# Zero blocks written by GpSimd instead of turned by TensorE, and five small re-orderings, in a one-core macaron block with stick-breaking attention

## The chip, the cores and the metric

The kernel runs on one core of a Trainium2 chip. Its time is the device time of one launch in microseconds (us), the median of several runs. Five engines work side by side, each through its own queue in order: PE (TensorE, matmuls and transposes), DVE (VectorE), ACT (ScalarE), POOL (GpSimd) and SP (SyncE, which issues the DMAs). Semaphores link them. "L1098" is line 1098 of the kernel before.

## The reference

One macaron block on x of 1024 rows by 1024 columns, all in float32: a gated FFN, stick-breaking attention with 16 heads of width 64, a second gated FFN.

```python
x = x + 0.5 * swiglu(rms_norm(x, n1), wi1, wo1)
x = x + stick_breaking_attention(rms_norm(x, mix_norm), w_qkv, q_gain, k_gain, w_o)
x = x + 0.5 * swiglu(rms_norm(x, n2), wi2, wo2)

# in the attention, for each head, t = row, s = column, s < t:
z = einsum("qd,kd->qk", rms_norm(q), rms_norm(k)) / sqrt(64)
# A[t,s] = sigmoid(z[t,s]) * prod over s<j<t of (1 - sigmoid(z[t,j]))
o = A @ v
```

## The kernel before

**Precision.** A float32 product is made of three matmuls: each operand is split into a high part (ACT copies it with rounding, L196) and a low part (DVE or POOL subtracts, L197), and high by high, low by high and high by low are added up in one bank of the accumulator (L308, L309, L310). For the weights w of the attention and for q and k a form with two matmuls is used (`th` and `tl`, `kh_s` and `kl_s`).

**Stages.** FFN 1 takes the first 620 us, a transition the next 140, the attention with the output projection behind it the time from about 700 to 1330, FFN 2 the rest.

**Attention.** The 16 heads run as 8 pairs (p = 0 to 7), some 63.5 us each. A pair has four units: `a` (head 1, rows 512 to 1023), `b` (head 0, rows 0 to 511), `c` (head 1, rows 0 to 511) and, already for the pair after it, `d` (head 0, rows 512 to 1023). Heads, rows and columns are stored mirrored, so that the product over j is a prefix scan. A unit does this:

- `scores` (L1058 to L1073): for each block `tb` of 128 rows, two matmuls make the scores in a bank `bz` (512 columns, or 512, 384, 256, 128 for the short blocks beside the diagonal). ACT takes two sigmoids of them, beta into `w` and 1 - beta back into the bank. A DVE scan (L1066) makes the running product, with `first` (zeros with a diagonal of ones) as the lower bound. POOL multiplies beta by it (L1073, the weights `w`), after a memset of the first column (L1071).
- `values`: for each group of 128-column blocks `sb`, `turn` transposes 128x128 pieces of `w` through the identity into a bank `bt` (L1098), and `split` makes `th` (ACT) and `tl` (DVE). `apply` multiplies them by v (L1116) into a bank `bo`. The last group of a unit holds two `sb`: one with two pieces, one with a single piece. The single piece is widened to two by a transpose of zeros from `first[:, P:2P]`, so that the matmul of `apply` has 256 columns for either. `th` and `tl` have two buffers each, so a group's tiles come free when the group two before it has been applied.

Between these stand the *fills*: 24 steps of the next pair's q, k, v projection (`qkv`, banks `bq`, L308 to L310), three matmuls of 384 columns for each of four 128-row slices of the contraction. When a projection tile is complete, ACT takes its squares and copies (L980, L981, L984), DVE reduces (L986), and after each four tiles `rsqrt` runs as one ACT instruction (`rs_a`, L207) and ten small DVE instructions (L208 to L212), followed by `r` (L992) and `f` (L1003). From `r` POOL scales k (L996, L999). `f` is the scale of the sigmoids. `prep_q` and `prep_k` then turn q or k (L1016) and multiply by the gains: ACT makes `q_s` or the high part `kh_s` (L1020), DVE the rest (`q_s` again, or `kl_s`, L1021).

**Order.** Every step goes into a list `plan` with a number for its place, and the list is sorted by that number. A unit's length is in `PARTS` (10, 14, 21, 16), and `put("c", 17.5, f)` means 17.5 after the start of `c`. `spread` sets steps at equal distances. Where an instruction of a queue stands follows from this list, except that `following(mark)` issues an instruction behind a named other one. The output weights (`out_weights`, tiles `raw`, 128x1024) are loaded during pair 6; the first two are copied on ACT at one place, near the end of unit `d` and the start of `a`. For the first pair no earlier unit exists, so its fills, `steps[12:]`, are spread over the numbers -30 to -11.

Of the kernel before, what the change touches and what calls it, by code (L numbers as in the profile page):

```python
# [9 lines left out]
F32 = mybir.dt.float32  # L10
F32R = mybir.dt.float32r
I32 = mybir.dt.int32
AF = mybir.ActivationFunctionType
# [100 lines left out]
def macaron_kernel(ctx, tc, x, g1, w1_in, w1_out, gm, w_qkv, gq, gk, w_o, g2, w2_in, w2_out, out):  # L114
# [801 lines left out]
    with ExitStack() as stack:  # L916
# [39 lines left out]
        def qkv(p, state):  # L956


            def start(half):
                if half:  # L960
                    state["v"] = pl[f"vst{p % 2}"].tile([P, NT, 4, DH], F32R, name="vst", bufs=1)
                state["qk", half] = pl[f"qk{half}"].tile([P, 4, 6, DH], F32, name=f"qk{half}", bufs=1)
                state["ssq"] = pl["sq"].tile([P, 4, 4], F32, name="ssq", bufs=1)

            def step(half, i, ks):
                if i == 0 and ks.start == 0:
                    start(half)
                if ks.start == 0:
                    state["ps"] = bank("bq")
                room, ps = state["ps"][:, 3 * P :], state["ps"][:, : 3 * P]  # L970
                wh, wl = state["wq"]
                t = rows(half * 4 + i)
                mm3(ps, [((xh[:, k, t], xl[:, k, t]), (wh[k], wl[k])) for k in ks], ks.start == 0, ks.stop == KD)
                if ks.stop == KD:
                    finish(half, i, ps, room)

            def finish(half, i, ps, room):
                qk, ssq, vst = state["qk", half], state["ssq"], state["v"]
                sq = pl["sq"].tile([P, 4, DH], F32, name="sq")
                act.activation(sq.rearrange("p a b -> p (a b)"), ps[:, : 2 * P], AF.Square)  # L980
                act.activation(qk[:, i, 0:4].rearrange("p a b -> p (a b)"), ps[:, : 2 * P], AF.Copy)  # L981
                pv = ps[:, 2 * P :].rearrange("p (a b) -> p a b", b=DH)
                vh = vst[:, half * 4 + i, 0:4:3, :]
                state["evacuated"] = act.activation(vh, pv, AF.Copy).ins  # L984
                dve.tensor_tensor(vst[:, half * 4 + i, 1:3, :], pv, vh.bitcast(F32), op=ALU.subtract)
                dve.tensor_reduce(out=ssq[:, i, :], in_=sq, axis=AX.X, op=ALU.add)  # L986
                if i < 3:
                    return
                y = rsqrt(pl["sq"], ssq.rearrange("p a b -> p (a b)"), 1.0 / DH, room[:, :16])
                y = y.rearrange("p (a b) -> p a b", b=4)  # L990
                r = state["r"] = pl["sq"].tile([P, 4, 4], F32, name="r", bufs=1)
                dve.tensor_scalar(r[:, :, 0:2], y[:, :, 2:4], 1.0, None, op0=ALU.mult)  # L992

                rk = r[:, :, 0:1].unsqueeze(3).to_broadcast([P, 4, 2, DH])
                kv = qk[:, :, 2:3, :].to_broadcast([P, 4, 2, DH])
                pool_e.tensor_tensor(qk[:, :, 4:6, :], kv, rk, op=ALU.mult)  # L996
                for to in (2, 3):
                    rk = r[:, :, 1:2].to_broadcast([P, 4, DH])
                    pool_e.tensor_tensor(qk[:, :, to, :], qk[:, :, 3, :], rk, op=ALU.mult)  # L999

                f = state["f", half] = pl["sq"].tile([P, 2, 4, 2], F32, name=f"f{half}")
                for n, c in enumerate((0.125, -0.125)):
                    dve.tensor_scalar(f[:, n], y[:, :, 0:2], c, None, op0=ALU.mult)  # L1003

            return [
                partial(step, half, i, ks)
                for half in (1, 0)
                for i in range(4)
                for ks in (range(0, 3), range(3, 6), range(6, KD))
            ]  # L1010
# [27 lines left out]
        def scores(state, hd, half):  # L1038

            w = state["w", hd, half] = {}  # L1040

            def step(tb, kb):
                L = T - tb * P
                if kb == half:
                    t = pl["w"].tile([P, T - tb % 4 * P], F32, name=f"w{hd}{tb % 4}", bufs=1)

                    om = t[:, L : 2 * L] if half else pl["om"].tile([P, T], F32, name="om")
                    state["om"], w[tb] = om, t[:, :L]
                om, wt = state["om"], w[tb]
                q = state["q", hd, half][:, (tb % 4) * P : (tb % 4 + 1) * P]  # L1050
                s0 = max(tb * P, kb * NHALF)
                n = (kb + 1) * NHALF - s0
                c0 = s0 - tb * P
                off = P if n == P else 0
                z = bank("bz")
                keys = slice(s0 - off - kb * NHALF, NHALF)
                for i in range(2):
                    pe.matmul(z[:, : off + n], q, state["k", hd, kb][i][:, keys], start=i == 0, stop=i == 1)  # L1058

                z = z[:, off : off + n]  # L1060
                for to, sign in ((wt[:, c0 : c0 + n], 0), (z, 1)):
                    marks["scored"] = act.activation(  # L1062
                        to, z, AF.Sigmoid, scale=state["f", half][:, sign, tb % 4, hd : hd + 1]
                    ).ins
                least = first[:, P : P + 1].to_broadcast([P, n]) if c0 else first[:, :n]
                dve.tensor_tensor_scan(  # L1066
                    om[:, c0 : c0 + n], z, least, initial=om[:, c0 - 1 : c0] if c0 else 0.0,
                    op0=ALU.mult, op1=ALU.max,
                )
                if c0 == 0:  # L1070
                    pool_e.memset(wt[:, 0:1], 0.0)  # L1071
                c1 = max(c0, 1)
                marks["weighed"] = pool_e.tensor_tensor(  # L1073
                    wt[:, c1 : c0 + n], wt[:, c1 : c0 + n], om[:, c1 - 1 : c0 + n - 1], op=ALU.mult
                ).ins

            return [partial(step, tb, kb) for tb in range(half * 4, half * 4 + 4) for kb in range(half, 2)]

        def values(state, p, hd, half):
# [8 lines left out]
            def turn(sbs):  # L1088
                w = state["w", hd, half]
                tp = bank("bt")  # L1090
                n, now_at = 0, tc.cur_priority
                for sb in sbs:
                    for i in range(max(blocks(sb), 2)):
                        c = (sb - tb0 - i) * P

                        src = w[tb0 + i][:, c : c + P] if i < blocks(sb) else first[:, P : 2 * P]
                        tc.cur_priority = now_at
                        pe.transpose(tp[:, n : n + P], src, ident)  # L1098
                        n += P
                th, tl = now[sbs] = [pl["th"].tile([P, NHALF], F32R, name=n) for n in ("th", "tl")]  # L1100
                split(tp[:, :n], th[:, :n], tl[:, :n])

            def apply(sbs):
# [76 lines left out]
        first = pl["first"].tile([P, NHALF], F32, name="first", bufs=1)  # L1180
        pool_e.memset(first, 0.0)
        dve.tensor_copy(first[:, :P], ident)
        spread(steps[12:], -30.0, -11.0)
        for p in range(-1, NP):
            this = states[p] if p >= 0 else None
            nxt = states[p + 1] if p < NP - 1 else None
# [19 lines left out]
            if nxt is not None:  # L1206
                if p >= 0:
                    fills = qkv(p + 1, nxt)
                    for part, span in PARTS.items():
                        for i in range(FILLS[part]):  # L1210
                            t = (span - (3.0 if part == "d" else 0.0)) * (i + 0.5) / FILLS[part]
                            put(part, t - 0.1 if (part, i) == ("a", FILLS["a"] - 1) else t, fills.pop(0))
                put("c", 15.0, partial(prep_q, nxt, 1))
                put("c", 17.5 if p >= 0 else 20.0, partial(prep_k, nxt, 0, 1))
                put("d", 8.0, partial(prep_k, nxt, 1, 1))
            if this is not None:
                put("a", 5.0, partial(prep_q, this, 0))
# [10 lines left out]
            if p == NP - 2:  # L1228

                def note(i, f):  # L1230
                    pool_e.tensor_tensor(seen[:, i : i + 1], f(), f(), op=ALU.mult)

                put("c", 14.0, partial(note, 0, lambda s=nxt: s["qk", 1][:, 0, 4, 0:1]))
                put("d", 1.0, partial(note, 1, lambda s=nxt: s["k", 0, 1][1][:, 0:1].bitcast(F32)))
                put("c", 10.0, partial(load_o, 1))
                put("d", 15.5, lambda: spots.append(tc.cur_priority))
            if p == NP - 1:
                put("a", 2.5, partial(load_o, 0))
                for at, _, _ in SHARES:
                    put(*at, lambda: spots.append(tc.cur_priority))  # L1240
# [10 lines left out]
    with pools(*PROJECTION) as pl:  # L1251
# [3 lines left out]
        def out_weights(c, k, rooms):  # L1255
# [9 lines left out]
                there = seen[:, k // 2 : k // 2 + 1] if k < 4 else wo[-1][1][:, 0:1].bitcast(F32)  # L1265
                pool_e.tensor_tensor((l_ if k < 4 else h_)[:, 0:1], there, there, op=ALU.mult)
            if c is HALVES[0]:
                split(raw, h_, l_, lane(f"wo{k // 2}"))
            else:
                with following(marks["scored"] if k < 4 else None):  # L1270
                    act.activation(h_, raw, AF.Copy)
# [113 lines left out]
```

## Time and profile before

| | us |
|---|---|
| median of 3 runs | 1916.08 (1914.53 to 1917.19) |
| profiled execution, its own time | 1914.4 |
| its span | 1912.5 |
| PE busy | 1897.4 (99%) |
| DVE, POOL, ACT busy | 1237.0, 1127.8, 979.9 |

The span runs from the first to the last instruction. The 1.9 us between span and time of the profiled execution lie around it. The granted clock was 1.0. In views of single instructions a row gives start, duration, engine, line and operation, output <- inputs, and in brackets how long the engine sat idle and who ended it. Matmuls are pipelined, so a row's duration overlaps the next one; what an instruction takes from PE is the step from its start to the next start.

### The profile page before, as it was taken

How to read it: one execution, taken by the hardware profiler on the slowest of the kernel's cores; microseconds unless marked ns; L12 is line 12 of the kernel's file. 1: busy time of each engine (PE TensorE's matmuls, PEld its weight loads, DVE VectorE, ACT ScalarE, POOL GpSimd, SP SyncE). 2: the span in 40 equal slices, each digit the busy share in tenths (PEclk: the TensorE clock that was granted, in tenths of full speed). 3: DMA queues.
4: the chain of work that ended last, by engine and by line, in shares of the span. 5: the costliest groups of instructions: out<-in, count | busy, mean ns of one | idle time of the engine just before them, and what ended most of it. 6: DMA issues, size and time to landing. Idle time of an engine off the chain costs nothing.

```text
span 1912.5 us, 26698 instructions
## 1 busy us (share of the span) xinstructions
PE 1897.4 (99%) x9362; PEld 1624.8 (85%) x9362; DVE 1237.0 (65%) x1713; ACT 979.9 (51%) x1794; POOL 1127.8 (59%) x999
## 2 busy tenths in 40 slices
PE   9999999999999999999999999999999999999999
PEld 8878888888888899999999897788888888888887
DVE  6856445535775758888888777568456445548645
ACT  7433433334335458878888876344433443434332
POOL 6766666656556746656665564215666666654554
PEclk9999999999999999999999999999999999999999
DMA  6233323338897411011111152612333323369983
GB/s 204 89 115 111 105 87 117 105 115 278 307 354 259 138 34 45 32 47 45 45 37 42 50 170 74 225 50 74 103 110 116 105 83 117 110 229 342 331 268 138
DMA packets 168982, 258.65 MB, mean 135 GB/s; under 512 B 11664, under 2 KB 82320, under 8 KB 168848
## 3 DMA queue, kind: packets, MB, share of 16 engines
q1 hardware_dynamic: 168704, 256.95, 39.3%
q8 instruction: 73, 1.20, 0.3%
q14 instruction: 61, 0.50, 0.1%
q10 hardware_dynamic: 144, 0.00, 0.0%
HBM read 197.14 MB, written 59.77 MB: 134 GB/s over the span
## 4 chain that ended last, share of the span: by engine, by line
PE 86%; DVE 8%; ACT 3%; issue 1%; POOL 1%; DMA 0%; SPq 0%; DVEq 0%; ACTq 0%; POOLq 0%
PE ka L308 6%; PE ka L309 6%; PE ka L310 6%; PE bq L308 4%; PE bq L309 4%; PE bq L310 4%; PE kc L308 4%; PE kc L309 4%; PE kc L310 4%; PE ma L310 4%; PE ma L309 4%; PE ma L308 4%; PE kb L308 4%; PE kb L309 4%; PE kb L310 4%; PE mb L310 3%
## 5 line engine op out<-in xcount | busy, mean ns | idle before, releaser
L197 POOL TENSOR_TENSOR rp<-raw,rp 128x1024 fp32r<-128x1024 f32 x84 | 213.7, 2551 | 168.0 <-ACT rp L196 157.0
L197 POOL TENSOR_TENSOR u<-sf,u 128x512 fp32r<-128x512 f32 x160 | 227.6, 1425 | 136.2 <-ACT u L196 136.2
L197 POOL TENSOR_TENSOR u<-raw,u 128x512 fp32r<-128x512 f32 x128 | 187.5, 1467 | 152.5 <-ACT u L196 151.7
L196 ACT ACTIVATE u<-sf 128x512 fp32r<-128x512 f32 x160 | 100.8, 630 | 204.7 <-PE kb L309 87.1
L1073 POOL TENSOR_TENSOR w<-w,om 128x512 f32<-128x512 f32 (+4 forms) x128 | 140.9, 1104 | 107.6 <-DVE om L1066 94.0
L446 DVE TENSOR_TENSOR h<-h 128x512 f32<-128x512 f32 x110 | 135.4, 1234 | 85.8 <-POOL h L554 85.1
L308 PE MATMUL bq<-wqh,xh 128*128 128x384 f32 x512 | 174.4, 341 | 0.4
L196 ACT ACTIVATE rp<-rh 128x1024 fp32r<-128x1024 f32 (+1 forms) x78 | 76.4, 983 | 189.9 <-issue 60.2
L309 PE MATMUL bq<-wql,xh 128*128 128x384 f32 x512 | 172.2, 336 | 0.0
L310 PE MATMUL bq<-wqh,xl 128*128 128x384 f32 x512 | 172.1, 336 | 0.0
L576 DVE TENSOR_TENSOR raw<-raw 128x1024 f32<-128x1024 f32 (+1 forms) x60 | 95.0, 1585 | 105.4 <-DMA raw<-w_out 91.7
L196 ACT ACTIVATE u<-raw 128x512 fp32r<-128x512 f32 x128 | 80.2, 630 | 149.8 <-PE ka L309 100.8
L308 PE MATMUL ka<-xh,u 128*128 128x512 f32 x352 | 137.2, 390 | 1.9 <-ACT s L499 1.9
L308 PE MATMUL ma<-rp 128*128 128x512 f32 x352 | 137.0, 389 | 0.0
L310 PE MATMUL ka<-xh,u 128*128 128x512 f32 x352 | 137.0, 389 | 0.0
L310 PE MATMUL ma<-rp 128*128 128x512 f32 x352 | 136.9, 389 | 0.0
L309 PE MATMUL ka<-xl,u 128*128 128x512 f32 x352 | 136.9, 389 | 0.0
L309 PE MATMUL ma<-rp 128*128 128x512 f32 x352 | 136.9, 389 | 0.0
L554 POOL TENSOR_TENSOR h<-h,g 128x512 f32<-128x512 f32 x80 | 113.0, 1412 | 35.1 <-DVE h L503 33.3
L1062 ACT ACTIVATE w<-bz,f 128x512 f32<-128x512 f32 (+1 forms) x192 | 113.1, 589 | 34.5 <-PE bz L1058 33.4
L475 DVE TENSOR_TENSOR sf<-raw 128x512 f32<-128x512 f32 x80 | 80.3, 1003 | 77.9 <-POOL u L197 77.9
L197 DVE TENSOR_TENSOR rp<-rh,rp 128x1024 fp32r<-128x1024 f32 (+1 forms) x70 | 109.7, 1585 | 21.9 <-ACT rp L196 19.6
(309 smaller groups left out, 5465.8 us busy)
## 6 DMA issues: line engine op xcount, KB each, us to landing
raw<-w_out SPq DMA_DIRECT2D x120, 512.0 KB, 5.7
raw<-w_in SPq DMA_DIRECT2D x86, 512.0 KB, 3.6
k<-h SPq DMA_DIRECT2D x154, 256.0 KB, 2.1
rh<-k SPq DMA_DIRECT2D x64, 512.0 KB, 6.2
raw_qkv<-w_qkv SPq DMA_DIRECT2D x64, 192.0 KB, 2.9
x_keep<-x SPq DMA_DIRECT2D x32, 256.0 KB, 3.4
x<-x_keep SPq DMA_DIRECT2D x32, 256.0 KB, 5.6
raw<-w_out SPq DMA_DIRECT2D x24, 256.0 KB, 4.6
```

Of the source, the lines that this page charges most:

```text
L196: first = act.activation(hi, raw, AF.Copy).ins
L197: return first, (engine or dve).tensor_tensor(lo, raw, hi.bitcast(F32), op=ALU.subtract).ins
L308: pe.matmul(dst, ah, bh, start=start and i == 0, stop=False, skip_group_check=onto)
L309: pe.matmul(dst, ah, bl, start=False, stop=False, skip_group_check=onto)
L310: pe.matmul(dst, al, bh, start=False, stop=stop and i == n - 1, skip_group_check=onto)
L446: dve.tensor_tensor(src, hb[of[0]], hb[of[1]], op=getattr(ALU, of[2]))
L475: dve.tensor_tensor(f[n], x, y, op=op)
L554: pool_e.tensor_tensor(h, h, gs[k], op=ALU.mult)
L576: dve.tensor_tensor(w[0], w[0], w[1], op=getattr(ALU, W_OF[m][2]))
L1062: marks["scored"] = act.activation(to, z, AF.Sigmoid, scale=state["f", half][:, sign, tb % 4, hd : hd + 1]).ins
L1073: marks["weighed"] = pool_e.tensor_tensor(wt[:, c1 : c0 + n], wt[:, c1 : c0 + n], om[:, c1 - 1 : c0 + n - 1], op=ALU.mult).ins
```

## The change

1. `turn` no longer transposes the zero block. Two POOL memsets write zeros into that block of `th` and `tl`, and `split` handles 384 columns instead of 512 in these groups (8 pairs by 4 units, so 32 groups).
2. `prep_k` of the next pair's (head 0, rows 512 to 1023) moves from 17.5 to 17.0 in `c`.
3. The fills of `d` are spread over 5.0 less than the unit's length instead of 3.0 less.
4. The first pair's fills are spread over -30 to -7.
5. The first two output-weight copies are issued behind a sigmoid at 3.0 and one at 9.0 in `b` of pair 6.
6. In the last pair, the scan of (head 1, `tb` 4), the first of `a`, is issued behind the instruction that makes `f`.

```diff
-                    dve.tensor_scalar(f[:, n], y[:, :, 0:2], c, None, op0=ALU.mult)
+                    state["rooted"] = dve.tensor_scalar(f[:, n], y[:, :, 0:2], c, None, op0=ALU.mult).ins
...
-                dve.tensor_tensor_scan(
+                with following(state["rooted"] if state is states[-1] and (hd, tb) == (1, 4) else None):
+                    dve.tensor_tensor_scan(
...
-                    for i in range(max(blocks(sb), 2)):
+                    for i in range(blocks(sb)):
...
-                        src = w[tb0 + i][:, c : c + P] if i < blocks(sb) else first[:, P : 2 * P]
-                        pe.transpose(tp[:, n : n + P], src, ident)
+                        pe.transpose(tp[:, n : n + P], w[tb0 + i][:, c : c + P], ident)
                         n += P
                 th, tl = now[sbs] = [pl["th"].tile([P, NHALF], F32R, name=n) for n in ("th", "tl")]
+                if blocks(sbs[-1]) == 1:
+                    for t in (th, tl):
+                        pool_e.memset(t[:, n : n + P].bitcast(F32), 0.0)
                 split(tp[:, :n], th[:, :n], tl[:, :n])
...
-        spread(steps[12:], -30.0, -11.0)
+        spread(steps[12:], -30.0, -7.0)
...
-                            t = (span - (3.0 if part == "d" else 0.0)) * (i + 0.5) / FILLS[part]
+                            t = (span - (5.0 if part == "d" else 0.0)) * (i + 0.5) / FILLS[part]
...
-                put("c", 17.5 if p >= 0 else 20.0, partial(prep_k, nxt, 0, 1))
+                put("c", 17.0 if p >= 0 else 20.0, partial(prep_k, nxt, 0, 1))
...
+                for k, at in ((0, ("b", 3.0)), (2, ("b", 9.0))):
+                    put(*at, lambda k=k: marks.update({f"wo{k}": marks["scored"]}))
...
-                split(raw, h_, l_, lane(f"wo{k // 2}"))
+                with following(marks.get(f"wo{k}")):
+                    act.activation(h_, raw, AF.Copy)
+                lane(f"wo{k // 2}").tensor_tensor(l_, raw, h_.bitcast(F32), op=ALU.subtract)
```

What this does to the queues is shown at three places. The first is POOL's queue near the end of a pair's `a`, where unit `a`'s last group is turned. `qk` is the projected q and k, `w_9938` (`w_9954` after the change) the weights of one row block. Before:

```order
435 L999 TENSOR_TENSOR qk_9417<-qk_9417,r 128x4x64
436 L1073 TENSOR_TENSOR w_9892<-w_9892 128x383
437 L999 TENSOR_TENSOR qk_9417<-qk_9417,r 128x4x64
438 L1071 MEMSET w_9938 128x1
439 L1073 TENSOR_TENSOR w_9938<-w_9938 128x255
440 L1071 MEMSET w_9993 128x1
```

After:

```order
469 L1074 TENSOR_TENSOR w_9908<-w_9908 128x383
470 L1072 MEMSET w_9954 128x1
471 L1103 MEMSET th 128x128
472 L1103 MEMSET tl 128x128
473 L1074 TENSOR_TENSOR w_9954<-w_9954 128x255
474 L1072 MEMSET w_10010 128x1
```

Two memsets of 128x128 now stand ahead of the 255-column weights. The second place is DVE's queue from the end of `c` to `d` and on to the next `a` of the same pair. `ssq` is the sum of squares, `kl_s` and `q_s` the finished k and q. Before, at the end of `c`, and then at the end of `d`:

```order
789 L1021 SCALAR_TENSOR_TENSOR q_s_9544<-bz,gq_sb,q_s_9544 64x512
790 L197 TENSOR_TENSOR tl<-bt,th 128x512
791 L197 TENSOR_TENSOR tl<-bt,th 128x384
792 L1021 SCALAR_TENSOR_TENSOR q_s_9547<-bz,gq_sb,q_s_9547 64x512
793 L1066 SCALAR_TENSOR_TENSOR om<-bz,first 128x128
794 L1021 SCALAR_TENSOR_TENSOR kl_s_9594<-bz,gk_sb,kh_s_9593 128x512
```

```order
807 L1066 SCALAR_TENSOR_TENSOR w_9767<-bz,first 128x256
808 L197 TENSOR_TENSOR tl<-bt,th 128x512
809 L197 TENSOR_TENSOR tl<-bt,th 128x384
810 L986 TENSOR_REDUCE ssq<-sq 128x4
811 L985 TENSOR_TENSOR vst<-bq,vst 128x128
812 L208 TENSOR_SCALAR bq<-rs_a 128x16
```

After, the same two places:

```order
789 L1021 SCALAR_TENSOR_TENSOR q_s_9558<-bz,gq_sb,q_s_9558 64x512
790 L197 TENSOR_TENSOR tl<-bt,th 128x512
791 L197 TENSOR_TENSOR tl<-bt,th 128x384
792 L1021 SCALAR_TENSOR_TENSOR kl_s_9589<-bz,gk_sb,kh_s_9588 128x512
793 L1021 SCALAR_TENSOR_TENSOR q_s_9561<-bz,gq_sb,q_s_9561 64x512
794 L1067 SCALAR_TENSOR_TENSOR om<-bz,first 128x128
```

```order
807 L1067 SCALAR_TENSOR_TENSOR w_9782<-bz,first 128x256
808 L986 TENSOR_REDUCE ssq<-sq 128x4
809 L985 TENSOR_TENSOR vst<-bq,vst 128x128
810 L208 TENSOR_SCALAR bq<-rs_a 128x16
811 L210 SCALAR_TENSOR_TENSOR rs_u<-bq,rs_a 128x16
812 L211 TENSOR_TENSOR rs_u<-rs_u,bq 128x16
813 L197 TENSOR_TENSOR tl<-bt,th 128x512
```

`kl_s` moved ahead of the second `q_s`, and the reduction with the start of `rsqrt` moved ahead of the two splits `tl`. The third place is ACT's queue at the start of pair 6's `a`. Before:

```order
1071 L196 ACTIVATE th<-bt 128x512
1072 L196 ACTIVATE raw<-raw 128x1024
1073 L1062 ACTIVATE w_11541<-bz,f_11086 128x512
1074 L1062 ACTIVATE bz<-bz,f_11086 128x512
1075 L196 ACTIVATE raw<-raw 128x1024
1076 L1121 ACTIVATE o_11145<-bo 64x512
```

After:

```order
1071 L196 ACTIVATE th<-bt 128x384
1072 L1062 ACTIVATE w_11565<-bz,f_11108 128x512
1073 L1062 ACTIVATE bz<-bz,f_11108 128x512
1074 L1124 ACTIVATE o_11167<-bo 64x512
1075 L1062 ACTIVATE w_11598<-bz,f_11108 128x384
1076 L1062 ACTIVATE bz<-bz,f_11108 128x384
```

The two copies `raw<-raw` are gone from this place; they stand in unit `b` of the pair now.

More of the change, by code (lines that the diff above doesn't have):

```diff
@@ L1065, in step @@
                 least = first[:, P : P + 1].to_broadcast([P, n]) if c0 else first[:, :n]
[L1066 to L1069, printed above, removed]
+                with following(state["rooted"] if state is states[-1] and (hd, tb) == (1, 4) else None):
+                    dve.tensor_tensor_scan(
+                        om[:, c0 : c0 + n], z, least, initial=om[:, c0 - 1 : c0] if c0 else 0.0,
+                        op0=ALU.mult, op1=ALU.max,
+                    )
                 if c0 == 0:
```

## The prediction

> **What bounds the kernel now.** I read the page's busy times first, then PE's waits by line and waited-for instruction, then the timeline at each place that the change touches.
>
> ```profile
> span 1912.5 us, 26698 instructions
> ## 1 busy us (share of the span) xinstructions
> PE 1897.4 (99%) x9362; PEld 1624.8 (85%) x9362; DVE 1237.0 (65%) x1713; ACT 979.9 (51%) x1794; POOL 1127.8 (59%) x999
> ```
>
> PE is idle for 15.1 us of the span, so time can leave in two ways only: PE issues less, or one of its few waits goes. Work taken off or put on the other engines counts only where PE waits for it. The waits (PE's line, what it waited for: total, times, longest):
>
> ```profile
> PE bz L1058 <- DVE kl_s L1021: 1.5, 7, 0.2
> PE mb L287 <- DVE x L622: 0.9, 2, 0.5
> PE bz L1016 <- POOL w L1071: 0.9, 1, 0.9
> PE bz L1058 <- DVE w L1066: 0.9, 3, 0.3
> PE bo L1116 <- DVE tl L197: 0.6, 1, 0.6
> PE bt L287 <- DVE xl L197: 0.5, 1, 0.5
> PE bo L1116 <- ACT th L196: 0.4, 1, 0.4
> ```
>
> Five of these seven rows lie in the attention, 4.3 us together. That is all that the moves can win, apart from restart losses that the idle column leaves out.
>
> **The zero turns.** 32 transposes leave PE. Their group, from the view by lines:
>
> ```profile
> L1098 PE MATMUL bt<-ident,first 128*128 128x128 f32 x32 | 8.7, 273 | 0.0
> ```
>
> 273 ns is the time through the array, and the next one starts long before. What one costs PE is the step between starts:
>
> ```profile
> 879.21 1.03 PE L1098 MATMUL bt<-ident,w 128*128 128x128 f32 x8
> ```
>
> Eight in 1.03 us, the last of them 0.27 long: (1.03 - 0.27) / 7 = 0.109 us a step. 32 x 0.109 = 3.5 us. It can be 8.7 at most, by the busy time, and 0 if PE waits right behind each of them. I take -3.5, since no idle time stands behind them in the group's row.
>
> The Trainium skill (TensorE: Matmul & The Clock Gate, Part 4: PE-mode transpose) gives a transpose about 275 ns in a kernel's context. The trace agrees with that as a duration, 273 ns. By the page alone the turns would be worth 32 x 0.275 = 8.8 us and the whole change 11.3 (an estimate), but the step measured here is 0.109.
>
> **The memsets.** 64 are added on POOL. The trace has one of that shape, and the place in a pair's `a` where two will stand:
>
> ```profile
> 0.73 0.20 POOL masks.py:197 MEMSET ident<- 128x128 f32 x1 [0.29 <-POOLq L1375]
> ```
>
> ```profile
> 900.50 0.74 POOL L1073 TENSOR_TENSOR w<-w 128x255 f32<-128x255 f32 x1 [0.57 <-DVE w L1066]
> ```
>
> 64 x 0.20 = 12.8 us of POOL, which is idle 41% of the span. At the shown place POOL idles 0.57 us for a scan, and two memsets take 0.40 of that. Behind them in POOL's queue stand the next weights, and PE's later turns wait for those. The memsets also wait themselves, for the apply two groups earlier to free `th` and `tl`. At this place that apply is the following row; it ends at 899.01, about 0.9 us before POOL would come to them, right ahead of its idle time.
>
> ```profile
> 898.51 0.50 PE L1116 MATMUL bo<-tl,vst 128*128 128x512 f32 x1
> ```
>
> PE needs the zeros only with the 256-column apply, over 1 us after the turn. I take 0; the ends are 0 (added work cannot gain) and +12.8 with every memset exposed. The 32 splits that shrink from 512 to 384 columns on ACT and DVE lie beside PE's work: 0 as well.
>
> **k's split at 17.0 (7 pairs).** k is turned some three fills earlier, and `kl_s` passes the second `q_s` in DVE's queue. Before, on DVE and then on PE:
>
> ```profile
> 872.20 0.76 DVE L1021 SCALAR_TENSOR_TENSOR q_s<-bz,gq_sb,q_s 64x512 fp32r<-64x512 f32 x1
> 872.99 0.42 DVE L1066 TENSOR_TENSOR_SCAN om<-bz,first 128x128 f32<-128x128 f32 x1
> 873.33 0.73 DVE L1021 SCALAR_TENSOR_TENSOR kl_s<-bz,gk_sb,kh_s 128x512 fp32r<-128x512 f32 x1
> ```
>
> ```profile
> 871.89 0.60 PE L1016 MATMUL bz<-ident,qk 128*128 128x128 f32 x4
> ...
> 873.50 0.48 PE L1058 MATMUL bz<-kh_s,q_s 128*128 128x512 f32 x1
> 873.82 0.39 PE L1058 MATMUL bz<-kl_s,q_s 128*128 128x512 f32 x1
> 874.05 0.34 PE L308 MATMUL bq<-wqh,xh 128*128 128x384 f32 x1
> ```
>
> The bank that the 512-column score at 873.50 takes is then released by `kl_s`. In `q_s`'s old place `kl_s` ends at 872.20 + 0.73 = 872.93. PE comes at about 873.4, one turn earlier than now. Slack 0.4, cost 0. If ACT's `kh_s` is late and `kl_s` runs one `q_s` later, it ends near 873.7, a wait of 0.3: 7 x 0.3 = +2.1 at worst. No wait of PE stands at this place, so nothing can be gained.
>
> **The fills of `d` (7 pairs).** They end about 1.8 earlier in plan units, so projection, squares and `rsqrt` come earlier, ahead of the last splits of `d`. There is a gain at the end of the next `a` and a price at the end of `d`. The gain, on PE and then DVE:
>
> ```profile
> 901.96 0.40 PE L1058 MATMUL bz<-kh_s,q_s 128*128 128x512 f32 x1
> 902.55 0.51 PE L1058 MATMUL bz<-kl_s,q_s 128*128 128x512 f32 x1 [0.20 <-DVE kl_s L1021]
> ```
>
> ```profile
> 894.80 0.17 DVE L211 TENSOR_TENSOR rs_u<-rs_u,bq 128x16 f32<-128x16 f32 x1
> ```
>
> The step there is 0.59, against 0.23 for the same instruction at 873.82: 0.36 lost, seven times. Three `rsqrt` instructions of 0.17 leave the queue ahead of `o`'s addition, so `kl_s` comes up to 0.5 earlier; PE itself comes 0.11 earlier by `a`'s own zero turn. Between 0 and 0.36 of the wait goes. I take 0.28, nearer the upper end since DVE's queue is full up to `kl_s`: -2.0.
>
> The price, from ACT's queue at the end of `d`:
>
> ```profile
> 890.00 0.39 ACT L980 ACTIVATE sq<-bq 128x256 f32<-128x256 f32 x1 [0.75 <-PE bq L310]
> ```
>
> Now ACT idles 0.75 us after the splits `th` and before the squares. Afterwards the squares, two copies and `rs_a` (which waits for DVE's reduction) go first, and the splits are late next: PE's applies and the following turn, which needs the bank, wait for them. One ACT instruction of 0.39 late is the upper end, 0 the lower, since the fills put in ahead may cover it. I take +0.3, seven times +2.1. The ends of the whole part: -2.5 and +2.7; the value 0.
>
> **The first pair's fills.** Two of PE's three waits for scans lie here:
>
> ```profile
> 702.32 0.38 PE L1058 MATMUL bz<-kh_s,q_s 128*128 128x256 f32 x1 [0.22 <-DVE w L1066]
> ...
> 706.58 0.39 PE L1058 MATMUL bz<-kh_s,q_s 128*128 128x256 f32 x1 [0.34 <-DVE w L1066]
> ```
>
> With fewer fills early, the scores stand closer together, but later ones get fills between. By their idle time the two are 0.56 us. I take -0.5; the ends are -1.0 (both, with restart losses) and +0.3 (a similar wait elsewhere, with `rsqrt` a microsecond later).
>
> **The two weight copies.** ACT's queue at the start of pair 6, and PE:
>
> ```profile
> 1083.43 1.06 ACT L196 ACTIVATE raw<-raw 128x1024 fp32r<-128x1024 f32 x1 [1.00 <-DMA raw<-w_o]
> ...
> 1085.54 1.06 ACT L196 ACTIVATE raw<-raw 128x1024 fp32r<-128x1024 f32 x1
> ```
>
> ```profile
> 1089.35 0.51 PE L1116 MATMUL bo<-th,vst 128*128 128x512 f32 x1 [0.44 <-ACT th L196]
> 1090.49 0.50 PE L1116 MATMUL bo<-tl,vst 128*128 128x512 f32 x1 [0.64 <-DVE tl L197]
> ```
>
> 2.1 us of copies, and a 1.00 us wait for the DMA, delay the sigmoids and the splits. PE loses 0.44, then a step of 1.14 against 0.23, so 0.91. Both go: -1.35. In `b` the copies may cost a little where `kh_s` follows one of them, +0.1 (0 to +0.4). Their subtractions wait on POOL, far behind. Together -1.3, between -1.5 and 0.
>
> **The last pair's scan.** On DVE, POOL and PE:
>
> ```profile
> 1149.08 1.22 DVE L1066 TENSOR_TENSOR_SCAN w<-bz,first 128x512 f32<-128x512 f32 x1
> ...
> 1152.96 0.16 DVE L992 TENSOR_SCALAR r<-bq 128x8 f32<-128x8 f32 x1
> ```
>
> ```profile
> 1153.42 1.50 POOL L996 TENSOR_TENSOR qk<-qk,r 128x512 f32<-128x512 f32 x1
> ```
>
> ```profile
> 1154.98 0.66 PE L1016 MATMUL bz<-ident,qk 128*128 128x128 f32 x4 [0.88 <-POOL w L1071]
> ```
>
> PE's wait of 0.88 for k hangs on `r`, which stands behind the scan of 1.22, `o`'s addition and a second scan. Rooted behind `f`, the scan lets `r` come near 1150, and L996 ends 2 us earlier: the 0.88 goes. The scan itself comes 0.9 us later, so the next 256-column score, which needs its bank, and then a split each wait a few tenths more. Net -0.8 (with restart loss); -1.5 to +0.3.
>
> **Sum.** -3.5 + 0 + 0 + 0 - 0.5 - 1.3 - 0.8 = -6.1 us. The profiled execution took 1914.4 us and would take 1908.3. It lies 1.7 below the median of the runs shown, 1916.08, from which the same subtraction gives 1910.0. About 0.2%, 3.8 us, is what a measurement can tell from no change.
>
> **The rivals.**
>
> *The moves eat the turns.* The end of `d` costs 0.4 per pair (+2.7), the end of `c` 0.3 (+2.1), and the wait at the end of `a` stays: -3.5 + 4.8 - 2.6 = -1.3, so 1914.8. For it: DVE's queue has no gap around either place. Against it: the slack of 0.4 at `c`. Chance 0.22.
>
> *The memsets make it slower.* They sit ahead of the weights in POOL's in-order queue. If a unit loses x us by them, the change brings 32x - 6.1: nothing is left from x = 0.19, and slower by 3.8 from x = 0.31. With both memsets exposed, x = 0.40, it is +6.7, so 1922.8. For it: POOL's memsets wait for PE's applies, a wait that did not exist. Against it: POOL's idle time at those places, as at 900.50. Chance 0.07.
>
> *The turns are worth their whole duration.* By the busy time, 8.7 instead of 3.5: -11.3, so 1904.8. The steps of 0.109 speak against it. It is what the page's 275 ns would give. Chance 0.04.
>
> That the change doesn't do what it says is excluded for the turns: the order of the changed kernel has none.
>
> **How the numbers follow.** The forecast has 0.67, with a range of its own from -9 (all ends of the moves favourable) to -3.5 (turns alone). The range 1906 to 1915 takes in the forecast without its last favourable microsecond and the first rival; outside lie the slower rival, the largest gain and some of the edges, under 2 in 10. Faster by over 0.2%: 0.62 of the forecast, the 0.04 and 0.02 of the first rival, 0.68. Slower: 0.07. Within: 0.25.
>
> **What would show it.** 32 fewer instructions on PE and no row with `first` on PE; PE's busy time lower by 3.5 in steps, though its sum by durations may fall 8.7; memset rows on POOL near 0.20 us, with no new PE wait for POOL. The waits for `tl` (0.6) and `th` (0.4) at 1089 to 1090 and for POOL at 1154.98 gone. The seven waits for `kl_s` at the end of `a` smaller, and new ones of at most 0.4 at the end of `d`, for `th` or `tl`. Wrong it would be if PE's waits for ACT and DVE grew by more than 2 us in the seven pairs, or if weights `w` came late behind memsets.

## The result and the profile after

| | before | after |
|---|---|---|
| median, us | 1914.74 (6 runs, 1914.24 to 1917.19) | 1905.30 (6 runs, 1904.93 to 1906.09) |
| profiled execution, us | 1914.4 | 1906.09 |
| ratio after / before | | 0.9948, interval 0.9937 to 0.9959 |

The change makes the kernel 9.4 us faster by the medians and 8.3 by the two profiled executions. Forecast were 6.1, and 1910.0 in a range of 1906 to 1915. The three runs of before on which the absolute number stood had a median of 1916.08; 27 later runs of before have 1914.58. The differences are the better bar, and there the forecast is 3.3 us short by the medians, 2.2 by the profiles. Of the 4.7 us between 1910.0 and 1905.30 the other 1.3 come from the base, 1916.08 against 1914.74.

The page of the profile after, its span and busy times (line numbers are those of the kernel that was run: L1116 of before is L1119 here, L1066 is L1067):

```profile
span 1904.3 us, 26681 instructions
## 1 busy us (share of the span) xinstructions
PE 1892.7 (99%) x9330; PEld 1620.3 (85%) x9330; DVE 1230.2 (65%) x1713; ACT 975.7 (51%) x1794; POOL 1138.2 (60%) x1063
```

PE has 32 instructions fewer and POOL 64 more, as built. PE's busy time fell by 4.7 us, its idle time from 15.1 to 11.6. PE's waits after the change:

```profile
PE ka L308 <- ACT s L499: 1.9, 2, 1.4
PE kc L691 <- POOL xl L685: 1.6, 1, 1.6
PE mb L287 <- DVE x L622: 1.5, 3, 0.5
PE bt L287 <- DVE xl L197: 0.5, 1, 0.5
PE kb L751 <- DVE xs L720: 0.4, 1, 0.4
PE bz L1016 <- DVE w L1067: 0.3, 1, 0.3
PE bt L308 <- ACT xh L196: 0.2, 1, 0.2
PE bz L1058 <- DVE w L1067: 0.2, 1, 0.2
```

The five attention rows that the prediction listed are gone or shrunk: the seven waits for `kl_s` (1.5), the wait for POOL before k's turns (0.9), those for `tl` (0.6) and `th` (0.4). Two waits for scans remain, 0.5 together.

**Where it came from.** The idle column leaves out what PE loses in restarting, so I counted lost time by steps. For each shape of matmul there is a usual step from start to start (the median: 0.227 us for 512 columns, 0.174 for 384, 0.119 for 256, 0.109 for a 128x128 transpose). What a step takes beyond that is lost. Both kernels make the same 192 scores in the same order, so the losses can be summed between the same scores:

| stretch | lost before | lost after | difference |
|---|---|---|---|
| up to the first score | 9.26 | 9.92 | +0.66 |
| first 8 scores | 1.17 | 0.59 | -0.58 |
| on to score 144 (pairs 0 to 5) | 9.82 | 7.71 | -2.11 |
| 144 to 152 (start of pair 6) | 1.85 | 0.28 | -1.57 |
| 152 to 168 (rest of pair 6) | 1.70 | 1.04 | -0.66 |
| 168 to 184 (last pair) | 4.41 | 4.03 | -0.38 |
| rest | 1.87 | 2.01 | +0.14 |
| sum | 30.08 | 25.58 | -4.50 |

With 32 x 0.109 = 3.49 us less to issue that is 7.99 of the 8.3 us.

In pairs 0 to 5 most of the gain, 1.7 of 2.11, lies at the end of `a`. There the fills' `rsqrt` ends earlier and `kl_s` with it. PE's 512-column score at that place, and then `kl_s` on DVE, in the pair that the prediction showed:

```profile
899.53 0.40 PE L1058 MATMUL bz<-kh_s,q_s 128*128 128x512 f32 x1
899.83 0.50 PE L1058 MATMUL bz<-kl_s,q_s 128*128 128x512 f32 x1
```

```profile
899.03 0.74 DVE L1021 SCALAR_TENSOR_TENSOR kl_s<-bz,gk_sb,kh_s 128x512 fp32r<-128x512 f32 x1
```

The step was 0.59 and is 0.30; `kl_s` ends at 899.77, just ahead of its use at 899.83. That is 0.29 a pair, and the prediction had 0.28.

At the end of `d` the prediction had a price of 0.3. ACT's queue there, and PE's:

```profile
886.21 0.38 ACT L980 ACTIVATE sq<-bq 128x256 f32<-128x256 f32 x1 [0.19 <-PE bq L310]
886.49 0.38 ACT L981 ACTIVATE qk<-bq 128x256 f32<-128x256 f32 x1
886.75 0.28 ACT L984 ACTIVATE vst<-bq 128x128 fp32r<-128x128 f32 x1
887.09 0.22 ACT L207 ACTIVATE rs_a<-ssq 128x16 f32<-128x16 f32 x1
887.21 0.97 ACT L196 ACTIVATE th<-bt 128x512 fp32r<-128x512 f32 x2
```

```profile
887.93 0.43 PE L1119 MATMUL bo<-th,vst 128*128 128x512 f32 x1
888.20 0.39 PE L1058 MATMUL bz<-kh_s,q_s 128*128 128x512 f32 x1
888.42 0.40 PE L1058 MATMUL bz<-kl_s,q_s 128*128 128x512 f32 x1
888.71 0.55 PE L1098 MATMUL bt<-ident,w 128*128 128x128 f32 x3
889.02 0.48 PE L1119 MATMUL bo<-tl,vst 128*128 128x512 f32 x1
```

The squares do go ahead of the splits, as forecast. But the squares no longer wait 0.75 us for their fill (0.19 now), and the chain of four runs while PE is still at the turns that the splits need. These turns and their first split, before (PE, ACT) and after (PE; its split is the last row of ACT's queue above):

```profile
887.08 0.93 PE L1098 MATMUL bt<-ident,w 128*128 128x128 f32 x7
888.27 0.98 ACT L196 ACTIVATE th<-bt 128x512 fp32r<-128x512 f32 x2 [0.18 <-PE bo L1116]
```

```profile
886.01 0.93 PE L1098 MATMUL bt<-ident,w 128*128 128x128 f32 x7
```

From the end of the seven turns to the first split pass 0.26 us before (888.01 to 888.27) and 0.27 after (886.94 to 887.21), so the splits are no later behind their turns. And between the apply of `th` (887.93) and that of `tl` (889.02) PE's queue holds a score and three turns that are ready. The turn at 888.71 starts 0.29 after the score, 0.06 late. No row has a wait. By the steps, PE loses 0.27 a pair over the scores of `d` and `a` together (8 of a pair's 24) after the change, and 0.36 before.

The memsets, as a group on POOL, and in the pair's `a` where the prediction looked for their room:

```profile
L1103 POOL MEMSET th<- 128x128 f32 x32 | 6.6, 207 | 14.0 <-DVE tl L197 9.0 <-PE bo L1119 4.2
```

```profile
897.26 0.20 POOL L1103 MEMSET th<- 128x128 f32 x1
897.40 0.20 POOL L1103 MEMSET tl<- 128x128 f32 x1
897.77 0.74 POOL L1074 TENSOR_TENSOR w<-w 128x255 f32<-128x255 f32 x1 [0.17 <-DVE w L1067]
```

They take 0.20 us each and start 0.14 apart, and POOL still idles 0.17 for the scan before the weights.

### The profile page after: what moved, and what is told of

Its sections match the earlier page's. It is cut to its first block, busy times and chain, and to the rows that moved or that the text cites. A ratio compares the mean times of both kernels' runs of the same rounds, so it can differ in the third digit from the quotient of the medians.

```text
span 1904.3 us, 26681 instructions
## 1 busy us (share of the span) xinstructions
PE 1892.7 (99%) x9330; PEld 1620.3 (85%) x9330; DVE 1230.2 (65%) x1713; ACT 975.7 (51%) x1794; POOL 1138.2 (60%) x1063
## 4 chain that ended last, share of the span: by engine, by line
PE 91%; DVE 6%; ACT 1%; issue 1%; POOL 1%; DMA 1%; SPq 0%; DVEq 0%; ACTq 0%; POOLq 0%
PE ka L308 6%; PE ka L309 6%; PE ka L310 6%; PE bq L308 5%; PE bq L310 5%; PE bq L309 5%; PE kc L309 4%; PE kc L308 4%; PE kc L310 4%; PE kb L309 4%; PE kb L310 4%; PE kb L308 4%; PE ma L308 4%; PE ma L310 4%; PE ma L309 4%; PE bz L1058 3%
```

## The experiments

All differences below are of medians, us, unless they are said to be lost time, which is counted by steps as above. The changed kernel run again beside the first three edits gave 1905.65 (1905.42 to 1906.39), 9.1 below the 1914.73 of before there.

**The changed kernel again.**

> The changed kernel once more, on the chip of the three runs beside it, as the bar for them. It stood 8.3 us below the kernel before by the two profiled executions and 9.4 by the medians. Expected 8 to 9.5 us below the kernel before.

1905.65, 9.1 below: inside.

**Fills of `d` back at 3.0.**

```diff
-(span - (5.0 if part == "d" else 0.0))
+(span - (3.0 if part == "d" else 0.0))
```

> The changed kernel with the fills of d back at 3.0. Theory A (the moved fills free the waits for kl_s at the end of a, about 0.28 in each of 7 pairs, and cost nothing at the end of d): 2.0 to 2.5 us slower than the changed kernel, and PE's row of 7 waits for kl_s comes back with some 0.2 us of idle time each. Theory B (the prediction's sum: the same gain, paid back at the end of d): within 0.5 us of the changed kernel, with the waits for kl_s back and waits of about 0.3 gone elsewhere. Theory C (the shorter splits and the missing turn freed the waits, not the fills): within 0.5 us, and the waits for kl_s stay away.

1908.91, 3.3 slower. In each of the five pairs from score 24 to 144 0.40 to 0.43 more is lost, by the two profiles of the changed kernel. It all lies at the end of `a` (0.40); the end of `d` is the same within 0.03. The row is back:

```profile
PE bz L1058 <- DVE kl_s L1021: 2.0, 6, 0.3
```

This is the mechanism of theory A, with a size above its range of 2.0 to 2.5. The prediction's payback (B) and the other cause (C) fall.

**Zero turns back on PE.** The old loop over `max(blocks(sb), 2)`, no memsets, splits of 512.

> The changed kernel with the 32 zero blocks turned by PE again, splits of 512 and no memsets; all moves stay. Theory A (a turn costs PE its step of 0.109 us): 3.5 us slower than the changed kernel. Rival (a turn costs its duration of 0.273): 8.7 us slower. A second rival (the longer splits bring waits at the end of a and d as well): 5 to 6 us slower, with rows of waits for th, tl or kl_s that the changed kernel does not have.

1909.91, 4.3 slower. From the first score on the traces have 3.9 to 4.2, by the two profiles of the changed kernel: 3.49 of steps and 0.5 to 0.7 of lost time, of which 0.27 lies at one score in `c` of pair 6 and 0.3 in the last pair. Theory A, with a little of the second rival there; the duration of 0.273 has no part in it.

**k's split back at 17.5.** `put("c", 17.5 if p >= 0 else 20.0, ...)`.

> The changed kernel with prep_k back at 17.5. Theory A (the move is free and brings nothing): within 0.5 us of the changed kernel, with no new PE wait. Rival (the move makes room that the earlier fills of d need): 1 to 3 us slower, with a wait in each of 7 pairs near the end of c or in d.

1905.79, 0.1 slower, no new wait in the pairs. Theory A.

The next four runs had other runs of before beside them, with 1914.49 instead of 1914.73. Counted by the distance to before, each is 0.24 slower than stated here.

**The two copies back at the start of `a`.** `split(raw, h_, l_, lane(...))` in place of the copy issued behind a mark.

> The changed kernel with the two out-weight copies back at the start of pair 6's a. Theory A (they delay ACT's sigmoids and splits there): 1.3 to 1.6 us slower than the changed kernel, and PE's waits for th and tl at the start of that a are back, 0.4 and 0.6 us of idle time. Theory B (other moves have made room for them): within 0.3 us.

1912.88, 7.2 slower, and both theories were far off. PE waits once, for 4.3 us, and loses 6.2 at the start of pair 6. ACT's queue there and PE's row of waits:

```profile
1079.51 1.06 ACT L196 ACTIVATE raw<-raw 128x1024 fp32r<-128x1024 f32 x1 [4.09 <-DMA raw<-w_o]
1080.47 0.20 ACT L207 ACTIVATE rs_a<-ssq 128x16 f32<-128x16 f32 x1
1080.58 0.96 ACT L196 ACTIVATE th<-bt 128x512 fp32r<-128x512 f32 x2
```

```profile
PE bo L1119 <- ACT th L196: 4.3, 1, 4.3
```

Here the copies have their old place in the plan, but with the fills at 5.0 the squares are ahead of it and `rs_a` and the splits behind: the copy now blocks both. Its DMA is issued at 1075.4, lands 4 to 5 us later, and ACT stands idle for 4.09 us. In the kernel before, the copy came behind the splits and waited 1.00.

**The hold behind `f` taken out.** `following(None)` around the scan.

> The changed kernel without holding the last pair's scan behind f. The prediction has 0.8 us for it; the two profiles show only 0.4 less lost PE time in the last pair. Theory A: 0.3 to 0.5 us slower, PE's wait of 0.9 us for POOL before k's turns back, some waits of 0.2 to 0.4 for scans and banks gone. Theory B (with the earlier fills rsqrt is early enough without it): within 0.2 us and no wait of 0.9.

1905.79, 0.1 slower than the changed kernel (0.4 by the distance to before), which doesn't part the theories. The trace is theory B: no wait of 0.9, and 0.15 to 0.2 more lost in the last pair. PE waits 0.3 for POOL (`qk`, L996) instead of 0.3 for a scan.

**First pair's fills to -11.**

> The changed kernel with the first pair's fills spread to -11 again. Theory A: the two waits for scans in the first pair, 0.22 and 0.34 of idle time, are back: 0.6 us slower than the changed kernel. Rival (they are gone for another reason): within 0.2 us, and no such wait.

1906.41, 0.8 slower; three waits for scans at L1058, 0.7 together, instead of one of 0.2. Theory A.

**Every memset four times.**

```diff
-                    for t in (th, tl):
+                    for t in (th, tl) * 4:
```

> The changed kernel with every memset of zeros made four times over: 256 instead of 64, so 1.66 us of POOL for each of the 32 groups instead of 0.41. It measures POOL's slack at those places. Theory A (POOL has over 1.3 us to spare there): within 0.5 us of the changed kernel. Theory B (the slack is some 0.4 to 0.6 us, as at the place that the prediction shows): about 0.7 us lost in each unit, 15 to 25 us slower, with PE waits for w of L1074 at its turns. Rival (only some units have no slack): 3 to 12 us slower, with these waits at one or two places of each pair.

1906.29, 0.6 slower. From the first score up to the last pair the losses are the same as in the changed kernel within 0.1 us. The two waits for POOL that came stand in the last pair:

```profile
1141.36 0.39 PE L1119 MATMUL bo<-tl,vst 128*128 128x256 f32 x1 [0.32 <-POOL w L1072]
...
1149.06 0.33 PE L1098 MATMUL bt<-ident,w 128*128 128x128 f32 x1 [0.47 <-POOL w L1072]
```

Theory A except for the last pair. Six more memsets, some 0.8 us by their starts, fit into POOL's slack at the groups of the other pairs, so the rival in which the memsets make the kernel slower had no ground.

The next three start from the kernel before.

**Fills at 5.0 alone.**

> The kernel before with only the fills of d at 5.0. Theory A (the moved fills gain some 2.5 to 3 us in 7 pairs, but put the first out-weight copy ahead of rs_a and the splits th in ACT's queue, where it waits for its DMA): a wait of PE for th of 4 us or more at the start of pair 6, 5 us more lost there than before, so 2 to 3 us slower than the kernel before. Theory B (the prediction: gain paid back at the end of d, copies as before): no change, within 0.5 us.

1917.97, 3.4 slower than before. Up to score 144 the pairs lose 2.2 less, then 4.4 more is lost at the start of pair 6 and 0.7 more in the last pair:

```profile
1081.35 1.06 ACT L196 ACTIVATE raw<-raw 128x1024 fp32r<-128x1024 f32 x1 [3.84 <-DMA raw<-w_o]
```

```profile
1083.05 0.65 PE L1116 MATMUL bo<-th,vst 128*128 128x512 f32 x1 [4.01 <-ACT th L196]
```

Theory A, 0.4 beyond its range; the 0.7 of the last pair was in no theory. Without the moved copies the fills make the kernel slower.

**Fills at 5.0 and the copies in `b`.**

> The kernel before with the fills of d at 5.0 and the two out-weight copies in b. Theory A (copies cleared out of the way, the fills keep their gain): 4 to 5 us faster than before, 2.5 to 3 from the pairs and 1.5 from pair 6, no wait for th over 0.3. Theory B (the prediction's terms): 1.3 us faster.

1911.37, 3.2 faster. It lies between the two theories. From score 24 to 144, the ends of `d` and of `a` in five pairs, 2.0 less is lost, 0.40 a pair: 0.31 around the end of `a`, 0.09 around the end of `d`. So the end of `d` gained a little instead of paying. Pair 6 has the gain at the end of `a` too, 0.34; what it gains at the end of its `d` can't be told from the copies there, and I count 0.1 as in the other pairs. Of the seven waits for `kl_s` one is left, in the first pair, whose fills are not those of a `d`:

```profile
PE bz L1058 <- DVE kl_s L1021: 0.2, 1, 0.2
```

The start of pair 6 gives 1.6, with the 0.1 for the end of `d` in it. The copies are not free at their new place: at the end of `b` of pair 6 two steps lose 0.30 to 0.34 together in each of the thirteen profiles with the copies in `b`, and 0.02 to 0.04 in the four with the copies at the old place. In the changed kernel `kl_s` (DVE) ends there at 1102.78, right ahead of the score (PE) that takes the bank it read; the step to that score is 0.31 instead of 0.12:

```profile
1102.04 0.74 DVE L1021 SCALAR_TENSOR_TENSOR kl_s<-bz,gk_sb,kh_s 128x512 fp32r<-128x512 f32 x1
```

```profile
1102.53 0.28 PE L1119 MATMUL bo<-tl,vst 128*128 128x256 f32 x1
1102.84 0.50 PE L1058 MATMUL bz<-kh_s,q_s 128*128 128x512 f32 x1
```

In the last pair 0.7 more is lost than before. PE's wait ahead of k's turns, 0.88 in the prediction's row, has grown:

```profile
1150.20 0.44 PE L1016 MATMUL bz<-ident,qk 128*128 128x128 f32 x2 [1.47 <-POOL qk L996]
```

**Turns replaced alone.**

> The kernel before with only the zero turns replaced by memsets. Theory A (0.109 for each turn, less the one of a, which only makes PE come earlier to its wait for kl_s): 2.7 to 3.5 us faster than before, with the 7 waits for kl_s grown from 0.2 to 0.3 us of idle time. Theory B (the shorter splits free the waits for kl_s as well): 5 us or more faster, those waits gone.

1910.49, 4.1 faster, between the ranges of A (2.7 to 3.5) and B (5 or more). The waits for `kl_s` grew as theory A has it, since PE comes to them earlier:

```profile
PE bz L1058 <- DVE kl_s L1021: 1.9, 6, 0.3
```

The 0.1 that each pair loses there it gets back at the end of `d`, and 0.5 us less is lost in pair 6 and the last pair. With the steps' 3.49 that makes 4.0. Theory B's sign, waits for `kl_s` gone, is not there.

**The sixth fill of `c` 0.6 later** (from the changed kernel).

```diff
-put(part, t - 0.1 if (part, i) == ("a", FILLS["a"] - 1) else t, fills.pop(0))
+put(part, t - 0.1 if (part, i) == ("a", FILLS["a"] - 1) else t + 0.6 if (part, i) == ("c", 5) else t, fills.pop(0))
```

> The changed kernel with the sixth fill of c put 0.6 later, behind two groups' applies and q's turns. In the changed kernel this fill loses 0.25 us in each pair: its bank bq is free only when f has been made. Theory A (the applies are ready to fill that time): 1 to 2 us faster than the changed kernel. Theory B (the second tl of these applies is ready only at about the same time): within 0.5 us, with waits for tl in place of those for the bank.

1904.88 (1904.43 to 1905.37), the fastest median of all. Against the two medians of the changed kernel, 1905.30 and 1905.65, it is 0.4 to 0.8 lower, which is too little to tell from these runs. In the trace 0.1 less is lost in each pair: between the theories.

Two questions were open after these: whether a price at the end of `d` exists at all, and what ends the wait of 1.47 in the last pair.

**Fills of `d` at 7.0** (from the changed kernel).

> The changed kernel with the fills of d at 7.0 instead of 5.0: the squares, rs_a and the reduction move ahead of the splits once more, and the late splits th and tl move behind them. Theory A (the price at the end of d exists, and 5.0 has just not reached it): 2 to 4 us slower than the changed kernel, with waits of PE for th, tl or the bank of w's turns of 0.3 to 0.5 in each of 7 pairs. Theory B (PE has other ready work to put between at 7.0 too): within 0.5 us, no new row of 7 waits.

1907.86, 2.2 slower. At the end of `d` 0.07 more is lost in a pair; most, 0.32, is lost at the end of `a`, where the old wait is back:

```profile
PE bz L1058 <- DVE kl_s L1021: 1.5, 6, 0.3
```

The time is theory A's, but neither theory placed the loss. The squares come earlier, but other work now stands between them and `r`: on ACT two splits `th` ahead of `rs_a` (886.04 to 887.12), on DVE two splits `tl` between the reduction and the first step of `rsqrt` (886.67 to 887.96) and a scan of 0.69 behind that step. So `r` comes later. From the squares to `r`, at 7.0:

```profile
885.76 0.39 ACT L980 ACTIVATE sq<-bq 128x256 f32<-128x256 f32 x1 [1.29 <-PE bq L310]
```

```profile
893.58 0.17 DVE L992 TENSOR_SCALAR r<-bq 128x8 f32<-128x8 f32 x1
```

and `r` in the changed kernel:

```profile
892.29 0.17 DVE L992 TENSOR_SCALAR r<-bq 128x8 f32<-128x8 f32 x1
```

That is 7.8 us from the squares to `r` at 7.0, and 6.1 (from 886.21) at 5.0. `o`'s addition, the split of `o` and in the end `kl_s` are late with it.

**Fills, copies and the hold** (from the kernel before).

> The kernel before with the fills of d at 5.0, the copies in b, and the last pair's scan held behind f. Without the hold this kernel has a wait of 1.5 us for POOL's scaling of k (L996) in the last pair. Theory A (the hold is what ends that wait): the wait falls to 0.5 or less, and the kernel is 0.8 to 1.3 us faster than the same one without it, 1910.2 to 1910.6. Theory B (the hold moves the wait to other places): the 1.5 goes, waits for scans and banks of about the same sum come, and the time stays within 0.3 us of 1911.4.

1910.43, 0.9 below the same kernel without the hold. Theory A: the 1.47 is gone, and this is left there:

```profile
PE bz L1016 <- DVE w L1067: 0.3, 1, 0.3
```

**Turns, fills and copies** (from the kernel before).

> The kernel before with the turns replaced, the fills of d at 5.0 and the copies in b; no hold, no change of k or of the first pair. If the parts add up (4.1 for the turns alone, 3.2 for fills and copies): 7.3 us below before. If the turns gain more once the waits at the end of a are gone (their 7 turns no longer run into them, 0.8): 8.1 us below. The wait of 1.5 for L996: there if only the hold removes it (Theory A of the run before), and at most 0.4 if the changed order after the turns removes it as well, as the changed kernel without the hold suggests (0.3).

1906.28, 8.35 below before: 4.1 and 3.2 alone, 1.0 more together. The trace has 7.9 from the first score on, near the second sum of 8.1. The wait for L996 is 0.3 here without the hold. So the hold and the replaced turns each end the same wait, and either is worth near nothing after the other.

## Why the prediction was wrong

**The step that failed** is the price in "the fills of `d`": "I take +0.3, seven times +2.1. The ends of the whole part: -2.5 and +2.7; the value 0". Measured, with the copies out of the way, the part is -0.40 in each of five pairs: -0.31 at the end of `a` (forecast -0.28) and -0.09 at the end of `d` (forecast +0.3; nothing beyond 0.03 in the changed kernel, where the turns are replaced as well). With as much in pair 6 that is -2.4; the seventh wait belongs to the first pair's fills. Taken out of the changed kernel the part is worth 2.8 to 3.0 by the lost time in pairs 1 to 7 and 3.3 by the medians, beyond the end of -2.5 that I gave. So a term forecast at 0 measured -2.4 to -3.3, which is most of the missing 3.3 us. The gain at the end of `a` was sized right; the price at the end of `d` was not there. I took most of one ACT instruction as the price because the squares pass the splits. I left out that the squares' own wait of 0.75 us ends earlier by that, so that they run while PE turns, and that PE has a score and a group of turns to issue before it needs `tl`.

The other steps:

- **Turns:** -3.5 forecast, 32 x 0.109 = 3.49 by the steps; 4.1 alone and 4.3 when undone, by medians. The group's busy time, 8.7, was the wrong measure: a queue of transposes pays the step. The 275 ns that the Trainium skill (TensorE: Matmul & The Clock Gate, Part 4: PE-mode transpose) gives for a transpose in one kernel's context, in a sentence on 128x128 bf16, agrees as a duration with the row here, 273 ns in float32, but does not hold as a price. (The prediction's 11.3 by that page should be 11.4: 8.8 and the 2.6 of the moves.)
- **Memsets:** 0 forecast, no loss found; with four times as many, 0.6.
- **k's split:** 0 forecast, 0.1 measured.
- **First pair:** -0.5 forecast, 0.8 when undone. The lost time has -0.58 in the first eight scores and 0.27 more behind them, at the first of the seven waits for `kl_s`, which the prediction had put to the fills of `d`.
- **Copies:** -1.3 forecast. Measured are -1.5 at their old place and +0.3 in `b` (forecast +0.1), so -1.2. What the prediction missed is that the part is also the condition of the fills: without it 7.2 is lost. Its sentence on the copies looked at the old order, where ACT waits 1.00 for the DMA, and not at what the moved fills put behind that wait.
- **The hold:** -0.8 forecast; 0.9 where the turns are still there, 0.1 in the changed kernel. The mechanism is right, but the term does not add to that of the turns. The last pair as a whole has -0.4.
- **Rest of pair 6:** 0 forecast, -0.66 measured. It is made of -0.29 at the end of `a`, the sixth wait for `kl_s`, which belongs to the fills; +0.3 at the end of `b`, the copies; and -0.56 at one score of `c`. At that score the turns alone bring -0.36, and the fills and copies -0.28 together; why before lost 0.35 more there in pair 6 than in other pairs stays open.

Re-sized by the lost time (turns, fills, first pair, copies, last pair, the score in `c` of pair 6): -3.5 - 2.4 - 0.8 - 1.2 - 0.4 - 0.6 = -8.9. The two profiles have -8.65 from the first score on (-4.50 - 0.66 - 3.49), the two medians of the changed kernel -9.1 and -9.4. The prediction's own range has a slip: the favourable ends of its terms add up to -10.0 (-3.5 - 2.5 - 1.0 - 1.5 - 1.5), not -9. That two other errors nearly cancel is luck: pair 6's `c` brought 0.6 that no term had, and the hold with the last pair 0.4 less than its 0.8.

The first rival, moves that eat the turns, fell at its own place: no wait at the end of `c` or `d`. The slower rival fell with the fourfold memsets, and the rival of the whole duration with the turns put back: 4.3, not 8.7.

## What to carry to other kernels

When a step is moved ahead in an in-order queue, price both sides of it: what now stands behind it, and what wait of its own disappears; then look whether the bounding engine has ready work before it needs the late one. Re-read every later instruction with a long wait (a copy behind a DMA) against the new order: here two copies that cost 1.5 us in the old order cost 6 to 7 in the new one, and an edit that gains 2.4 us made the kernel 3.4 slower until they were moved. Terms that end the same wait must not be added. And more is not always better: fills moved to 5.0 gained 3.3 us over 3.0, at 7.0 only about 1.0 of that was left.

## What the runs showed of the hardware that was not expected

Runs of kernels that do the same up to the first score differ there. PE's lost time before the first score was 9.3 us in the profile of before and 11.35 in that of the kernel with the turns alone. The row that grew, from 0.9 in 2 waits, reads in the latter:

```profile
PE mb L287 <- DVE x L622: 1.8, 4, 0.5
```

Of the difference, 2.0 lie between 580 and 720 us, around the transition. That is up to 2 us between single profiled executions, and more than several of the parts are worth. The sums between like scores repeat far better: from score 24 to 144 the two profiles of the changed kernel have 6.67 and 6.52, 0.03 apart in a pair.
